# Summed weights made by VectorE instead of an adding DMA, the pre-norm weights loaded with x's first piece, and the products with v half a step later

## The chip, the cores and the metric

The kernel runs on one NeuronCore of a Trainium2 chip. The metric is the device time of one execution in microseconds (us). It was measured over several executions; one more was profiled, and its trace gives the rows below. Engines: TensorE (PE, its weight loads PEld), VectorE (DVE), ScalarE (ACT), GpSimd (POOL), and SyncE (SP), which here only issues DMAs.

## The reference

One encoder layer on 256 tokens of width 2048, all in float32. After a root-mean-square norm, one wide projection makes the inputs of a gated linear recurrence (branch A), of a windowed attention with 16 heads (branch B), of their gates and of two merge gates:

```python
xn = rms_norm(x, norm_pre_w[l])
z = xn @ w_in[l]
u_lru, g_lru, q, k, v, g_attn, m_lru, m_attn = jnp.split(z, split_at, axis=-1)
...
y_a = h.astype(x.dtype) * jax.nn.silu(g_lru)
...
y_b = windowed_gqa(q, k, v, attn_sink[l]) * jax.nn.silu(g_attn)
merged = (jax.nn.sigmoid(m_lru) * (y_a @ w_proj_a[l])
          + jax.nn.sigmoid(m_attn) * (y_b @ w_proj_b[l]))
x = x + rms_norm(merged @ w_out[l], norm_post_w[l])
```

`rms_norm` divides by the root of the mean square of a row and multiplies by a weight for each column.

## The kernel before

**Arithmetic.** A float32 product is made of three products of a reduced type: an operand is split into a high part (a cast, by ScalarE, L219 for weights, L148 for other tiles) and a low part (value minus high part, by VectorE, L221 and L149), and TensorE sums high x high, high x low and low x high (L225 to L227 and their relatives). So each weight passes DMA, ScalarE and VectorE before TensorE reads it.

**The order of the work** is written out by hand. `START`, `MERGE` and `OUT` are lists of steps, one per 128x2048 block of weights (1 MB). A name is a group letter, a part and an index: `p` and `b` are the products with `w_proj_a` and `w_proj_b`, `o` those with `w_out`, `u` and `v` parts of the first projection. A step has two halves of 128x1024. In the steps named by a small letter a half is a tick of the schedule; in the steps L, M, N, A and O both halves make one. The loop at L1136 goes through the halves; at half number hs it issues the work due at its tick, then the cast of half hs + 4, the subtraction of half hs + 3, then the matmuls of half hs. Each engine works through its own queue in that order. Weights land in three 1 MB buffers (`raw`), loaded three steps ahead by SP's queue.

**Seven products instead of eight.** Groups L, M, N, A and O (class `Seven`) compute two by two blocks of an output from seven block products. Some multiply a single block of the activations, some a sum of blocks, and the weights of some are sums too:

```python
    "m5": ("s1", "x", (0, 1)),
    "m3": ("s4", "y", (1, 1)),
    "m6": ("s2", "x", (1, 1)),
    "m7": ("s3", "y", (0, 1)),
    "m4": ("a22", "x", (1, 0)),
```

The second entry names a cell (two 128x1024 tiles a and b, for each half q of the contraction). A cell starts as one block of weights and other blocks are added one after the other: x is the block of m1, then that of m5, m6 and m4 are added; y is the block of m3, then m7's is added. So m6 adds to x the block (1, 1), which is also what y holds when m3 is split. In the kernel before, each addition is a DMA issued on POOL's queue that adds what it reads from DRAM to the tile (`load(..., add=True)`, L192), asked for five steps ahead (`lead == 5`, L374), after the previous value of the tile has been split. The tiles are named after group, cell and half: `Ax0a` is group A, cell x, q = 0, half a.

Groups A and O stand in these lists:

```python
    b0.0 Am5.1 b0.1 Am3.0 b0.2 b0.3 Am3.1 b1.0 Am6.0 b1.1 b1.2 Am6.1 b1.3 Am7.0 b2.0 b2.1 Am7.1 b2.2 Am4.0 b2.3 b3.0
OUT = """o2.0 o2.1 Om1.1 o2.2 Om5.1 Om2.0 o2.3 Om3.0 Om6.0 Om3.1 o3.0 Om6.1 Om2.1 o3.1 Om7.0 Om7.1 Om4.0 Om4.1
    o3.2 o3.3""".split()
```

**Behind a product pb** (steps b, `add_pb`), VectorE multiplies each token half of its sums by a gate and adds the other branch (L970 and L971, tile `sm`); one tick later TensorE transposes the result (`turn`, L982, tile `mt`), 128x128 at a time, which ScalarE and VectorE split for the last product. o2's sums are evacuated by ScalarE (L1080) and VectorE (L1085).

**Attention heads** (`head`) run beside the steps. Two heads share a transposition through DRAM: `send`, `fetch` (DMAs), `p_parts` (split into `ph` and `pl`), `values` (the six products with v, PSUM bank `o`), `gate_out` (VectorE, `sga`, L927); `yb_parts` splits the gated result for the pb products. Their ticks are offsets from the head's first tick: `p_parts` at 11, `values` at 13, `gate_out` at 14.

**Shared space.** SBUF tiles of 4 KB a partition come from a pool of 45 units; PSUM has four banks of one kind and two double banks of another.

**The start.** TensorE first spins on ones (`SPIN` matmuls, L449). ScalarE's queue issues the DMA of x's first 128 columns (transposed), then the first 16 columns of `pvec`, the pre-norm weights, then the second piece of x; SP's queue issues the other pieces of x and the first weights in small parts. `scale_x` (L479, L481) multiplies a piece of x by the norm's weights and splits it. The norm's division by the row's root comes later (`row_scale`, at tick 10), from the squares of the four tiles of x (`square`, L499); its result is kept in `rbc`.

Of the kernel before, what the change touches and what calls it, by code (L numbers as in the profile page):

```python
# [28 lines left out]
EPS = 1e-6  # L29
UNITS = 45  # L30
DECAY = 12
SPIN = 11
HEAD0 = -16
HEADS_AT = (0, 3, 5, 8, 11)
FIRST = 8
# [34 lines left out]
LRU = (-4, 0, 2, 2, 2, 2, 2, 4)  # L70
QUADS = {"u": ("w_in", U0), "v": ("w_in", V0), "p": ("w_proj_a", 0),
         "b": ("w_proj_b", 0), "o": ("w_out", 0)}
PAIRS = {"g": GL0, "h": GA0, "w": U0, "k": K0, "q": Q0}
SEVENS = {"L": ("w_in", ML0 + 1024), "M": ("w_in", ML0), "N": ("w_in", MA0), "A": ("w_in", MA0 + 1536), "O": ("w_out", 0)}


PV_NORM = 0
PV_CW = 16
PV_CB = PV_CW + 64
PV_BR = PV_CB + 16  # L80
PV_BI = PV_BR + 32
# [2 lines left out]
PV_N = PV_SINK + 16  # L84
# [28 lines left out]
    return {k: n for n, k in enumerate(dict.fromkeys(content(p) for p in load_plan()))}  # L113


def body(ctx, tc, x, xT, wall, wlru, pvec, npost, ident_d, mask_d, rope_d, out):
    nc = tc.nc
    const = ctx.enter_context(tc.tile_pool(name="const", bufs=1))
    units = ctx.enter_context(tc.tile_pool(name="units", bufs=UNITS))
# [35 lines left out]
    plan = load_plan()  # L155
# [6 lines left out]
    def at(hs, fn):  # L162
        assert hs >= now[0], (hs, now[0])
        due.setdefault(hs, []).append(fn)
# [15 lines left out]
    flat = lambda t: t.rearrange("p a b -> p (a b)") if len(t.shape) == 3 else t  # L180
# [15 lines left out]
    groups = {}  # L196
# [12 lines left out]
    def split(q, c=0, w=1024, cast=nc.scalar.copy, only=None):  # L209
        i, h = q // 2, q % 2  # L210
        if i >= len(plan):
            return
        if c == 0 and only != "l":
            parts[q] = [unit(f"w{s}{i}_{h}", F32R, (P, 1024)) for s in "hl"]
        wh, wl = parts[q]
        cell = groups[plan[i][1]].cell(*plan[i][2:]) if chained(i) else raws[i]
        hs, ls, raw = wh[:, c:c + w], wl[:, c:c + w], flat(cell[h])[:, c:c + w]
        if only != "l":
            cast(hs, raw)  # L219
        if only != "h":  # L220
            nc.vector.tensor_tensor(ls, raw, hs.bitcast(F32), ALU.subtract)  # L221

    def mm3(ps, wh, wl, xh, xl, start, stop, more=False):

# [118 lines left out]
    class Seven:  # L343
# [22 lines left out]
        def fetch(self, p, lead):  # L366
            m, q = p[2:]
            fresh = ("m1", "m3") if self.sums is None else ()
            if self.sums is None:
                if lead == 4 and m in fresh:  # L370
                    self.start(self.where(m), q)
                if lead == 4 and SEVEN[m][0][0] == "s":
                    self.kept[m, q] = x_sum(f"{self.name}{m}{q}", SEVEN[m][0], q)
            if lead == 5 and m in (("m5", "m6", "m7", "m4") if self.sums is None else ("m6", "m7", "m4")):  # L374
                load(self.cell(m, q), p, True)

        def start(self, where, q):
# [63 lines left out]
    pv = const.tile([P, PV_N], F32, name="pv")  # L441
# [5 lines left out]
    spin = bank("spin", (P, 512))  # L447
    for _ in range(SPIN):
        nc.tensor.matmul(spin[:, 0:P], ones, ones, start=True, stop=True)  # L449
    nc.gpsimd.memset(warm, 0.0)  # L450
    nc.gpsimd.memset(eps, EPS)
    norm = lambda k: pv[:, PV_NORM + k:PV_NORM + k + 1]
    ident = const.tile([P, P], F32, name="ident")
    rbc = const.tile([P, S], F32, name="rbc")

    xt = [unit(f"xT{i}") for i in range(4)]
    xs = []
    raw_tile(0)
    for j in range(4):
        (nc.scalar if j < 2 else nc.sync).dma_start(xt[0][:, j], xT[0, :, j])  # L460
        if j == 0:
            nc.scalar.dma_start(pv[:, 0:PV_CW], pvec[:, 0:PV_CW])
        nc.sync.dma_start(raws[0][j // 2][:, j % 2 * 512:(j % 2 + 1) * 512], wall[0, :, j * 512:(j + 1) * 512])
    for i in (1, 2):
        for j in (0, 2):
# [3 lines left out]
            for c in ((0, 512), (512, 1024)) if i == 1 else ((0, 1024),):  # L469
                nc.sync.dma_start(raws[i][j // 2][:, slice(*c)], wall[i, :, j * 512 + c[0]:j * 512 + c[1]])  # L470
    nc.sync.dma_start(xt[3], xT[3])
    nc.sync.dma_start(pv[:, PV_CW:PV_N], pvec[:, PV_CW:PV_N])
    nc.scalar.activation(warm, warm, AF.Sigmoid)

    def scale_x(i, j, between=lambda: None):
        if j % 2 == 0:
            xs.append(pair_unit(f"xs{2 * i + j // 2}"))
        h, l = xs[-1][:, j % 2, 0], xs[-1][:, j % 2, 1]
        nc.scalar.activation(h, xt[i][:, j], AF.Copy, scale=norm(4 * i + j))  # L479
        between()  # L480
        nc.vector.scalar_tensor_tensor(l, xt[i][:, j], norm(4 * i + j), h.bitcast(F32), ALU.mult, ALU.subtract)  # L481

    for j in range(4):
        if j == 0:
# [375 lines left out]
    def head(hd, qh, ql, b, both, end):  # L860

        g, j = hd // 4, hd % 4
        sk = pv[:, PV_SINK + hd:PV_SINK + hd + 1]
        ts = [slice(t * P, (t + 1) * P) for t in range(2)]
        v = {}

        def scores():
            v["sc"] = bank(f"sc{hd}")
            for t in range(2):
                mm3(v["sc"][:, t], qh[:, j, ts[t]], ql[:, j, ts[t]], kv["kh"][:, g], kv["kl"][:, g], True, True)  # L870

        def expo():
            p = v["p"] = half_unit(f"p{hd}", ("p", "uu")[hd % 2])
            sc = v.pop("sc")
            m, nm, es = tiny(f"m{hd}"), tiny(f"nm{hd}"), tiny(f"es{hd}")
            dn = v["dn"] = tiny(f"dn{hd}")
            for t in range(2):
                nc.vector.tensor_tensor_reduce(p[:, t], sc[:, t], table["mask"][:, t], rtok_sc[:, t:t + 1], sk, ALU.add, ALU.max, m[:, t:t + 1])
            nc.vector.tensor_scalar(nm, m, -1.0, None, ALU.mult)
            soon(lambda: exps(p, nm, es, dn))  # L880

        def exps(p, nm, es, dn):
            for t in range(2):
                nc.scalar.activation(p[:, t], p[:, t], AF.Exp, bias=nm[:, t:t + 1], accum_out=dn[:, t:t + 1])
            nc.scalar.activation(es, nm, AF.Exp, bias=sk)
            v["es"] = es

        def normalise():
            dn, rd = v["dn"], tiny(f"rd{hd}")
            nc.vector.tensor_tensor(dn, dn, v["es"], ALU.add)  # L890
            nc.vector.reciprocal(rd, dn)
            soon(lambda: [nc.scalar.activation(v["p"][:, t], v["p"][:, t], AF.Copy, scale=rd[:, t:t + 1]) for t in range(2)])

        def flip():

# [13 lines left out]

        def fetch():  # L910
            u = both["l"] = unit(f"pl{hd}", F32R, (P, 1024))
            nc.sync.dma_start(u.bitcast(F32), both.pop("d").rearrange("c i t a x -> (c i) (t a x)"))

        def p_parts():
            both["h"] = unit(f"ph{hd}", F32R, (P, 1024))
            parts_of(both["h"], both["l"], both["l"].bitcast(F32))

        def values():
            both["o"] = bank(f"o{hd}")
            ks = slice(g * P, (g + 1) * P)  # L920
            turned = [both[i].rearrange("p (a h k x) -> p h k a x", a=8, h=2, k=2) for i in "hl"]
            for kt in range(2):
                mm3(both["o"], kv["vh"][:, kt, ks], kv["vl"][:, kt, ks], *(t[:, :, kt] for t in turned), kt == 0, kt == 1)

        def gate_out():
            y = sga[g][:, j - 1:j + 1]
            nc.vector.tensor_tensor(y, both["o"], y, ALU.mult)  # L927
            both.clear()
            if j == 3 and g < 2:
                soon(lambda: park("yb", sga, g), 4)  # L930

        for d, fn in ((0, scores), (1, expo), (3, normalise), (5, flip)):
            at(b + d, fn)
        if j % 2 == 1:
            for d, fn in enumerate((send, None, fetch, None, None, p_parts, None, values, gate_out), 6):
                if fn:
                    at(b + d, fn)
            if g > 1:
                at(max(b + 15, end + hd // 2 - 4), lambda: yb_parts(hd // 2))

    def yb_parts(q):
        yb[q] = pair_unit(f"yb{q}")
        n = q % 2 * 2
        parts_of(yb[q][:, :, 0], yb[q][:, :, 1], sga[q // 2][:, n:n + 2])
# [125 lines left out]
    b, n = ticks(), ticks(len(plan))  # L1070
# [159 lines left out]
```

## Time and profile before

| | |
|---|---|
| runs before | 880.4 us median of 3 (878.27 to 880.61) |
| profiled execution | 880.26 us, span 878.5 us |
| mean granted TensorE clock | 0.995 |
| DMA moved | 252.12 MB, mean 287 GB/s |
| HBM read, written | 232.43 MB, 18.87 MB |

The span goes from the first to the last instruction of the kernel. Busy shares are averages over the whole span. In a row of a timeline stand the start (us from the span's start), the time, the engine, the line, the operation, the tiles as out<-in, the shape, the count, and in brackets the engine's idle time before it with what ended it. In a row of the waits stand engine, line and what was waited for, then the total in us, the count and the longest. A matmul's time in the trace overlaps the next one's. The times of DMAs are told as us from issue to landing.

### The profile page before, as it was taken

The page shows a single profiled execution, that of the slowest core. Times are in us where ns is not written, and L with a number is a line of the kernel's source. Part 1 is how long each engine was busy: PE and PEld are TensorE (multiplying, and loading weights), DVE is VectorE, ACT ScalarE, POOL GpSimd, SP SyncE. Part 2 cuts the span into 40 slices and gives each one's busy share as a digit, 9 for nine tenths or more (in the row PEclk, how much of TensorE's full clock was granted, in tenths as well). Part 3 has the DMA queues.
Part 4 walks back from the last instruction along what each step waited for, and adds up shares of the span by engine and source line. Part 5 has one row for each costly group of instructions (what it writes and reads, how often), then busy time and mean ns, then how long its engine had stood idle before and what let it go on. Part 6 is the DMA issues. An engine that isn't in the chain of part 4 may idle for free.

```text
span 878.5 us, 12340 instructions
## 1 busy us (share of the span) xinstructions
PE 867.7 (99%) x4480; PEld 744.2 (85%) x4480; DVE 720.4 (82%) x967; ACT 643.2 (73%) x929; POOL 72.7 (8%) x104
## 2 busy tenths in 40 slices
PE   9999999999999999999999999999999999999996
PEld 9888888888888888888888888788888788888885
DVE  6899999898897988889777788987688578777776
ACT  7689687977788796886877699976566456555654
POOL 0000000012000011100001100000001001000200
PEclk9999999999999999999999999999999999999998
DMA  8757699999959999986999987899989998999962
GB/s 333 273 192 248 197 370 236 369 323 290 332 180 307 317 283 316 303 323 210 269 361 304 309 269 259 313 333 292 324 324 324 345 300 246 304 288 391 247 177 96
DMA packets 64685, 252.12 MB, mean 287 GB/s; under 512 B 6512, under 2 KB 19568, under 8 KB 49136
## 3 DMA queue, kind: packets, MB, share of 16 engines
q1 hardware_dynamic: 52384, 208.59, 64.1%
q0 software_dynamic: 11520, 41.95, 24.4%
q10 hardware_dynamic: 720, 0.79, 0.3%
q8 instruction: 35, 0.57, 0.3%
q14 instruction: 26, 0.21, 0.1%
HBM read 232.43 MB, written 18.87 MB: 286 GB/s over the span
## 4 chain that ended last, share of the span: by engine, by line
PE 84%; ACT 5%; DMA 5%; issue 4%; DVE 2%; POOLq 0%; POOL 0%; ACTq 0%; DVEq 0%
PE ga L252 7%; PE gl L252 7%; PE u L252 5%; DMA raw<-wall_dram 5%; PE Mm L407 4%; PE Lm L407 4%; PE gl L250 3%; PE ga L250 3%; PE Am L407 3%; PE Om L407 3%; PE q L252 3%; PE pb__6875 L272 3%; PE u L250 3%; PE u_ps L550 3%; PE pa__6035 L272 2%
## 5 line engine op out<-in xcount | busy, mean ns | idle before, releaser
L221 DVE TENSOR_TENSOR wl<-raw,wh 128x1024 fp32r<-128x1024 f32 (+1 forms) x252 | 299.1, 1202 | 71.2 <-ACT wh L219 55.5
L219 ACT CAST wh<-raw 128x1024 fp32r<-128x1024 f32 (+1 forms) x251 | 253.7, 1036 | 77.1 <-DMA raw<-wall_dram 51.9
L252 PE MATMUL ga<-xs,wh 128*128 128x512 f32 x256 | 63.5, 391 | 0.0
L252 PE MATMUL gl<-xs,wh 128*128 128x512 f32 x256 | 63.4, 391 | 0.0
L252 PE MATMUL q<-xs,wh 128*128 128x512 f32 x256 | 63.2, 391 | 0.0
L252 PEld LDWEIGHTS gl<-xs,wh 128*128 128x128 f32 x256 | 47.0, 188 | 9.1
L252 PEld LDWEIGHTS q<-xs,wh 128*128 128x128 f32 x256 | 47.0, 188 | 9.0
L252 PEld LDWEIGHTS ga<-xs,wh 128*128 128x128 f32 x256 | 46.7, 188 | 8.8
L252 PE MATMUL u<-xs,wh 128*128 128x512 f32 x192 | 47.5, 391 | 0.0
L252 PEld LDWEIGHTS u<-xs,wh 128*128 128x128 f32 x192 | 35.2, 188 | 6.7
L250 PEld LDWEIGHTS q<-xs,wl 128*128 128x128 f32 x256 | 33.2, 191 | 1.2
L250 PE MATMUL q<-xs,wl 128*128 128x256 f32 x256 | 34.0, 283 | 0.0
L250 PEld LDWEIGHTS ga<-xs,wl 128*128 128x128 f32 x256 | 33.0, 191 | 1.2
L250 PEld LDWEIGHTS gl<-xs,wl 128*128 128x128 f32 x256 | 32.8, 191 | 1.2
L250 PE MATMUL ga<-xs,wl 128*128 128x256 f32 x256 | 33.5, 283 | 0.0
L250 PE MATMUL gl<-xs,wl 128*128 128x256 f32 x256 | 33.2, 283 | 0.0
L250 PEld LDWEIGHTS u<-xs,wl 128*128 128x128 f32 x192 | 24.6, 191 | 0.9
L250 PE MATMUL u<-xs,wl 128*128 128x256 f32 x192 | 24.9, 283 | 0.0
L655 DVE SCALAR_TENSOR_TENSOR uu<-upad,pv,uu 128x256 f32<-128x256 f32 x48 | 23.2, 483 | 1.7
L739 ACT ACTIVATE sig<-sg 128x512 f32<-128x512 f32 x16 | 10.2, 636 | 14.2 <-DVE sg L582 14.2
L272 PE MATMUL pb__6875<-wh,yb 128*128 128x512 f32 x64 | 18.4, 413 | 0.0
L227 PE MATMUL gate<-ul,lwl 128*128 128x256 f32 x64 | 18.1, 283 | 0.0
(502 smaller groups left out, 2085.5 us busy)
## 6 DMA issues: line engine op xcount, KB each, us to landing
raw<-wall_dram SPq DMA_DIRECT2D x121, 1024.0 KB, 7.9
lraw<-wlru_dram SPq DMA_DIRECT2D x8, 512.0 KB, 6.3
away<-xx SPq DMA_DIRECT2D x8, 512.0 KB, 8.3
Lm<-away SPq DMA_DIRECT2D x8, 512.0 KB, 12.3
Mm<-away SPq DMA_DIRECT2D x8, 512.0 KB, 13.6
Nm<-away SPq DMA_DIRECT2D x8, 512.0 KB, 14.5
turn<-pt SPq DMA_DIRECT2D x32, 128.0 KB, 4.6
pl<-turn SPq DMA_DIRECT2D x8, 512.0 KB, 7.8
```

Source lines behind the costliest of these rows:

```text
L219: cast(hs, raw)
L221: nc.vector.tensor_tensor(ls, raw, hs.bitcast(F32), ALU.subtract)
L227: nc.tensor.matmul(ps, wl, xh, start=False, stop=stop, skip_group_check=more)
L250: nc.tensor.matmul(ps[:, 1], wl[:, sl], a[:, 0], start=False, stop=False)
L252: nc.tensor.matmul(ps, wh[:, sl], a, start=k == 0, stop=k == KT - 1)
L272: nc.tensor.matmul(got[t], a[:, i], (wl if low else wh)[:, sl], start=k + low + i == 0, stop=low == 1 and k == KT - 1)
L407: nc.tensor.matmul(self.ps[b], a[i], (wl if low else wh)[:, sl], start=fresh and j + low + i == 0, stop=last and j + low == 2, skip_group_ ...
L550: nc.tensor.matmul(ups[b // 2][:, b % 2, m], w[:, sl], a[:, n], start=k == 0 and w is wh and m == 0, stop=stop)
L655: nc.vector.scalar_tensor_tensor(u, up[:, j, tap:tap + S], cw[:, tap:tap + 1], u, ALU.mult, ALU.add)
L739: nc.scalar.activation(sg, dst, AF.Sigmoid)
```

## The change

1. For groups A and O, m6's block is no longer added by DMA. When the half of m3 is split, VectorE also adds this half (the tile of cell y) to the tile of cell x, right behind the subtraction. Eight adding DMAs of 128x1024 fall away (A and O, q = 0 and 1, halves a and b) and eight VectorE additions of 128x1024 come in. Groups L, M and N stay as they are.
2. The 16 columns of pre-norm weights move from `pvec` into a new array `x0`, behind x's first 128 columns (transposed), so that one DMA of 272 columns brings both into a tile `piece`. Its first 256 columns are `rbc`, written only later by the norm. `scale_x` reads x's first piece there; GpSimd copies it into its place in `xT` for the squares. ScalarE's queue issues one DMA less. `pvec` is loaded whole, by the DMA that loaded its rest.
3. `SPIN` goes from 11 to 8.
4. `values` and `gate_out` move from 13 and 14 to 14 and 15 ticks behind the head's first, and the earliest tick of `yb_parts` from 15 to 16.

```diff
-SPIN = 11
+SPIN = 8
...
+ADDED = {'A': {'m3': 'm6'}, 'O': {'m3': 'm6'}}
...
-PV_NORM = 0
-PV_CW = 16
+PV_CW = 0
...
         if only != "h":
             nc.vector.tensor_tensor(ls, raw, hs.bitcast(F32), ALU.subtract)
+            if plan[i][0] == "part" and plan[i][2] in ADDED.get(plan[i][1], ()):
+                x = flat(groups[plan[i][1]].cells["x", plan[i][3]][h])
+                nc.vector.tensor_tensor(x, x, raw, ALU.add)
...
-            if lead == 5 and m in (("m5", "m6", "m7", "m4") if self.sums is None else ("m6", "m7", "m4")):
+            if lead == 5 and m in ("m5", "m6", "m7", "m4")[self.sums is not None:] and m not in ADDED.get(self.name, {}).values():
                 load(self.cell(m, q), p, True)
...
-    norm = lambda k: pv[:, PV_NORM + k:PV_NORM + k + 1]
-    rbc = const.tile([P, S], F32, name="rbc")
+    piece = const.tile([P, S + KT], F32, name="rbc")
+    rbc = piece[:, 0:S]
+    norm = lambda k: piece[:, S + k:S + k + 1]
...
     for j in range(4):
-        (nc.scalar if j < 2 else nc.sync).dma_start(xt[0][:, j], xT[0, :, j])
         if j == 0:
-            nc.scalar.dma_start(pv[:, 0:PV_CW], pvec[:, 0:PV_CW])
+            nc.scalar.dma_start(piece, x0)
+        else:
+            (nc.scalar if j == 1 else nc.sync).dma_start(xt[0][:, j], xT[0, :, j])
         nc.sync.dma_start(raws[0][j // 2][:, j % 2 * 512:(j % 2 + 1) * 512], wall[0, :, j * 512:(j + 1) * 512])
...
-    nc.sync.dma_start(pv[:, PV_CW:PV_N], pvec[:, PV_CW:PV_N])
+    nc.sync.dma_start(pv, pvec)
+    nc.gpsimd.tensor_copy(xt[0][:, 0], rbc)
...
-        nc.scalar.activation(h, xt[i][:, j], AF.Copy, scale=norm(4 * i + j))
+        src = xt[i][:, j] if i + j else rbc
+        nc.scalar.activation(h, src, AF.Copy, scale=norm(4 * i + j))
         between()
-        nc.vector.scalar_tensor_tensor(l, xt[i][:, j], norm(4 * i + j), h.bitcast(F32), ALU.mult, ALU.subtract)
+        nc.vector.scalar_tensor_tensor(l, src, norm(4 * i + j), h.bitcast(F32), ALU.mult, ALU.subtract)
...
-            for d, fn in enumerate((send, None, fetch, None, None, p_parts, None, values, gate_out), 6):
+            for d, fn in enumerate((send, None, fetch, None, None, p_parts, None, None, values, gate_out), 6):
                 if fn:
                     at(b + d, fn)
             if g > 1:
-                at(max(b + 15, end + hd // 2 - 4), lambda: yb_parts(hd // 2))
+                at(max(b + 16, end + hd // 2 - 4), lambda: yb_parts(hd // 2))
```

More of the change, by code (lines that the diff above doesn't have):

```diff
@@ L113, in wall_rows, with body @@
     return {k: n for n, k in enumerate(dict.fromkeys(content(p) for p in load_plan()))}
-def body(ctx, tc, x, xT, wall, wlru, pvec, npost, ident_d, mask_d, rope_d, out):
+def body(ctx, tc, x, x0, xT, wall, wlru, pvec, npost, ident_d, mask_d, rope_d, out):
     nc = tc.nc
@@ L1199 @@
     pvec = np.concatenate([
-        cols(v["norm_pre_w"][0], 16),
         v["conv_w"][0].reshape(4, 16, P).transpose(2, 1, 0).reshape(P, 64),
@@ L1211 @@
         "x": x,
+        "x0": np.concatenate([x.T[:P], cols(v["norm_pre_w"][0], 16)], axis=1),
         "xT": x.T.reshape(4, 4, P, S).transpose(0, 2, 1, 3),
```

## The prediction

> **What bounds the kernel now.** I read the page first, then the waits of TensorE, then the two places where it stood still. On the page TensorE is busy for 99% of the span, so the other engines matter only where they make it wait.
>
> ```profile
> PE 867.7 (99%) x4480; PEld 744.2 (85%) x4480; DVE 720.4 (82%) x967; ACT 643.2 (73%) x929; POOL 72.7 (8%) x104
> q1 hardware_dynamic: 52384, 208.59, 64.1%
> q0 software_dynamic: 11520, 41.95, 24.4%
> PE mt L982 <- DVE sm L971: 1.8, 2, 0.9
> PE o L226 <- DVE pl L149: 0.6, 1, 0.6
> ```
>
> The last two lines are all that TensorE waits for between its first spin and its last product: 1.8 us before transposes of the merged rows, 0.6 us before a product of the softmax weights with v. So what the change can gain is these waits, what follows from them, and the start.
>
> The first wait, in the timeline of TensorE:
>
> ```profile
> 696.97 1.07 PE L407 MATMUL Am<-wh,Am 128*128 128x512 f32 x4
> 700.76 0.44 PE L982 MATMUL mt<-ident,sm 128*128 128x128 f32 x2 [0.91 <-DVE sm L971]
> 702.09 0.44 PE L982 MATMUL mt<-ident,sm 128*128 128x128 f32 x2 [0.89 <-DVE sm L971]
> 702.28 1.62 PE L272 MATMUL pb__6875<-wh,yb 128*128 128x512 f32 x4
> ```
>
> Two waits of 0.91 and 0.89 us, and then four products that take 1.62 us. Views of stretches (columns: length, busy time and count of each engine, granted clock, DMA share, GB/s) say why, and what the DMA did before:
>
> ```profile
> 652.00:676.00 24.00, 24.00 (x107) 19.75 (x106) 19.82 (x23) 18.69 (x23) 3.49 (x4) 1.00 1.04 342
> 676.00:700.00 24.00, 23.85 (x106) 19.42 (x104) 13.33 (x13) 10.25 (x12) 3.49 (x4) 1.00 1.04 348
> 700.00:704.00 4.00, 2.35 (x9) 1.82 (x10) 3.96 (x5) 2.39 (x5) 0.00 (x0) 0.85 1.04 305
> 704.00:708.00 4.00, 4.00 (x14) 3.16 (x14) 3.93 (x7) 1.20 (x2) 1.76 (x2) 0.72 1.03 291
> ```
>
> The granted clock falls to 0.85 and 0.72 in two stretches of 4 us: 4 x 0.15 + 4 x 0.28 = 1.72 us of matmul time lost, as much as the waits themselves. Together the place costs 1.80 + 1.72 = 3.52 us. And all DMA engines are full (1.04) for the 48 us before it. The chain of waits and VectorE's timeline lead from the transposes back to a load:
>
> ```profile
> 668.49 2.72 PE pb__6627 L272 x12
> 676.88 20.11 DMA raw<-wall_dram
> 697.06 1.06 ACT wh L219
> 699.29 0.69 DVE sm L970
> ```
> ```profile
> 693.16 1.23 DVE L221 TENSOR_TENSOR wl<-Ay1a,wh 128x1024 fp32r<-128x1024 f32 x1 [1.52 <-ACT wh L219]
> 698.15 1.23 DVE L221 TENSOR_TENSOR wl<-raw,wh 128x1024 fp32r<-128x1024 f32 x1 [2.49 <-ACT wh L219]
> ```
>
> The weights of step b1.0 were asked for at 676.88 and landed 20.11 us later, at 697.0. ScalarE's cast and VectorE's subtraction (698.15) had to wait for them, and the multiplication that feeds the transposes stands behind this subtraction in VectorE's order: it could have begun when TensorE ended the product pb0 and went on to a step of Am (696.97, so about 697.1), and began at 699.29, 2.2 us late. So the stall is a late DMA, in a stretch where the DMA is full.
>
> **The change, part by part.**
>
> *Sums for m6 by VectorE, group A.* The four halves of m6 of group A are no longer loaded and added by DMA. They are issued on POOL's queue here, first and last of the four:
>
> ```profile
> 655.02 0.89 POOL L192 DMA_DIRECT2D Ax0a<-wall_dram  x1 [33.44 <-DVE wl L221]
> 673.19 0.86 POOL L192 DMA_DIRECT2D Ax1b<-wall_dram  x1 [4.62 <-DVE wl L221]
> ```
>
> All four stand ahead of or beside the load of 676.88. Their price: queue q0 took 24.4% of 878.5 us = 214.4 us of all 16 engines for 41.95 MB, that is 80 halves of 0.524 MB, 2.68 us each; q1 took 563.1 us for 208.59 MB, 1.42 us for as much. An added half costs nearly twice a plain one. Four of them: 10.7 us of full DMA time gone before 697. Since the DMA is full throughout, loads behind them can land up to 10.7 us sooner. What is needed is only the 2.2 us by which the multiplication was late: a fifth of the relief is enough. Bounds: 0 (the load lands no earlier) and 3.52 us. I take 3.4: next in line are the second token half's sums. VectorE does four operations of 0.69 us from 697.1 on and ends about 699.9, just when TensorE has done the twelve products of Am (2.72 us from 696.97) and comes to the transposes; I leave 0.1 us for that.
>
> *What VectorE does instead*: eight additions of 128x1024, four for A, four for O. The same operation on the same engine has these rows:
>
> ```profile
> 811.30 3.50 DVE L221 TENSOR_TENSOR wl<-raw,wh 128x1024 fp32r<-128x1024 f32 x3
> L221 DVE TENSOR_TENSOR wl<-raw,wh x61: 1180/1219/1227, 639.4 to 839.9; 128x1024 fp32r<-128x1024 f32 x61
> 825.58 0.69 DVE L1085 TENSOR_TENSOR yw<-o__7602,np 128x512 f32<-128x512 f32 x1 [1.55 <-ACT junk L1080]
> 828.45 0.68 DVE L1085 TENSOR_TENSOR yw<-o__7602,np 128x512 f32<-128x512 f32 x1
> 834.18 1.07 PE L272 MATMUL o<-wh,ms 128*128 128x512 f32 x4
> ```
>
> Three in a row take 3.50 us and one 1.22, so one more costs (3.50 - 1.22) / 2 = 1.14 us; eight: 9.1 us, VectorE from 720 to 730 us. On the path they cost nothing if these covers hold. In A the two additions of q = 1 stand behind the subtraction of 693.16 and its like for half b: 2.3 us, in front of VectorE's idle 2.49 us before 698.15, so they fit even if no load came sooner. In O they stand behind the four Oy subtractions. Queued behind them are the evacuations of o2, at 825.58 and 828.45; for it waits the second PSUM tile of o3, whose first product is at 834.18. Margin 834.18 - 829.13 = 5.05 us; four additions are 4.6 us at most. The casts of Ox now wait for VectorE, not for a DMA. The four O loads give back another 10.7 us of DMA time, but TensorE waits for none there: gain 0, with the cover that it makes up for the earlier pace. Without it the lateness would be that of a half, 2.68 us at most, before the loads behind it. POOL's next additions (m7) wait 1.1 us more each for VectorE's reading of y, in front of a queue that is shorter by 10.7 us.
>
> *The products with v half a step later.*
>
> ```profile
> 565.67 0.40 PE L225 MATMUL o<-ph,vh 128*128 128x512 f32 x1
> 566.66 0.51 PE L226 MATMUL o<-pl,vh 128*128 128x512 f32 x1 [0.59 <-DVE pl L149]
> 565.38 1.23 DVE L149 TENSOR_TENSOR pl<-pl,ph 128x1024 fp32r<-128x1024 f32 x1
> L149 DVE TENSOR_TENSOR yb<-sga,yb x4: 679/684/684, 672.7 to 679.6; 128x512 fp32r<-128x512 f32 x4
> L272 PE MATMUL pb__6627<-wh,yb x64: 389/389/397, 668.3 to 696.3; 128*128 128x512 f32 x64
> ```
>
> TensorE came to the product at 565.67, its low part was ready at 566.6. Half a step (twelve products, 2.7 us) later TensorE comes at about 568.4, 1.8 us after it. The wait of 0.59 us goes; the clock did not fall after it, so that is all: bounds 0 and 0.59, I take 0.59. Moved with it, eight times: six products, one VectorE multiplication, a PSUM bank and two SBUF units held 2.7 us longer, and twice the store of yb on SP's queue. The last yb (started at 679.6) is ready some 2.7 us later, about 683, and its first use is the last half step of pb0, which begins 2.7 us before 696.97. Nothing of that is on the path; uncovered, a unit held longer takes at most half a step, 2.7 us, from a cast's lead.
>
> *The start.* The first weights of x no longer wait for a second small DMA.
>
> ```profile
> 0.75 0.41 ACTq L460 DMA_DIRECT2D xT<-xT_dram  x1
> xT<-xT_dram ACTq DMA_DIRECT2D x1, 128.0 KB, 3.5
> 1.19 0.45 ACTq L462 DMA_DIRECT2D pv<-pvec_dram  x1
> pv<-pvec_dram ACTq DMA_DIRECT2D x1, 8.0 KB, 4.0
> 1.00 5.06 PE L449 MATMUL spin<-ones 128*128 128x128 f32 x22 [1.00 <-POOL eps L451]
> 5.23 0.51 ACT L479 ACTIVATE xs<-xT,pv 128x256 fp32r<-128x256 f32 x1 [1.58 <-DMA pv<-pvec_dram]
> 21.61 1.05 ACT L219 CAST wh<-raw 128x1024 fp32r<-128x1024 f32 x1 [0.28 <-DMA raw<-wall_dram]
> 24.59 1.23 DVE L221 TENSOR_TENSOR wl<-raw,wh 128x1024 fp32r<-128x1024 f32 x1 [0.67 <-ACT wh L219]
> 24.92 2.17 PE L550 MATMUL u_ps<-xs,wl 128*128 128x256 f32 x16
> ```
>
> x's first piece was asked for at 0.75 and landed 3.5 us later, at 4.25; pv, asked for at 1.19, at 5.2. So the scaling can begin at about 4.3, 0.9 us sooner, and eight spins end at 1.00 + 8 x 0.46 = 4.7, just before the first product (4.85). But the gain doesn't last: in the group of 24.92 the second eight products use the low weights that VectorE finishes at 24.59 + 1.23 = 25.82, while TensorE reaches them at 25.87. That subtraction goes back through ScalarE's order (cast, square, cast, each 1.05) to a landing at 21.6, before which ScalarE idled 0.28 us. An earlier start turns into waits there unless the landing comes sooner, and the DMA loses only 8 KB of work. Bounds 0 and 0.9; I take 0.1. POOL's new copy of x's first piece is used by the first square, after 15 us.
>
> By the Trainium skill (TensorE: Matmul & The Clock Gate, Part 1) the clock is released only by a free-running window of about 3.4 us of sustained activity. Eight spins are 3.7 us, so by that rule the release could slip by a window; that is the third rival below.
>
> **Sum.** 3.4 + 0.59 + 0.1 = 4.1 us. The profiled execution took 880.26 us, 0.1 below the median of the runs (880.4): 880.26 - 4.1 = 876.2 us.
>
> **Rivals.**
> 1. *The relief does not reach the load* (or reaches it by less than 2.2 us): the queue refills with loads that are asked for sooner. For it: the DMA stays at 1.04 after 700, too. Against: the removed halves are a fifth of the 48 us ahead. Then 880.26 - 0.7 = 879.6, or 877.9 if only the clock's fall is spared.
> 2. *The start passes through*: the landing at 21.6 moves with everything else. For it: ScalarE idles 0.28 us before it. Against: the DMA, full by then, sets it. 876.2 - 0.8 = 875.4.
> 3. *The clock is released late at the start*: a stretch as after 702, 1.72 us lost, of which 0.9 is covered by the earlier start: 876.2 + 0.8 = 877.0. Against: products follow the spins within 0.2 us.
> 4. *Slower: VectorE falls behind in O.* Place: the second half of o3.0 at 834.18. If an addition costs far more than 1.14 us, because POOL issues four loads in this very stretch, the evacuation of o2 comes after its margin of 5.05 us plus VectorE's idle 1.5. It decides from 1.65 us per addition. At twice 1.2 us: 9.7 - 6.6 = 3.1 us of wait and, after a wait of that size, 1.7 us of clock: 876.2 + 4.8 = 881.0. Against: 61 operations of this shape, beside POOL's issues or not, all took 1.18 to 1.23 us.
>
> **How the numbers follow.** Forecast 0.64, rival 1 0.15, rivals 2 and 3 0.06 each, rival 4 0.09. The likeliest case has 875.3 (the start gives all, no remainder) to 877.1 (one wait of 0.9 left). The three runs before lie 2.3 us apart, and the range reaches half way into rival 1: 874.8 to 878.8. A measurement of this kernel tells 0.3%, 2.6 us, from no change. Faster: 0.64 + 0.12 = 0.76; within: 0.15; slower: 0.09.
>
> **What would show it.** Right: no wait of mt on sm near 697, clock 1.00 in that stretch, the raw load of b1.0 landing before 694; no wait of o on pl; the first product at about 4.9, and new waits of TensorE before 26 us that eat 0.8 of it; q0 with 72 halves, 37.7 MB. Wrong: TensorE waiting for wl or for PSUM after 818, VectorE's additions over 1.3 us, or the clock below 1 after 10 us.

## The result and the profile after

The kernel after takes 876.76 us (median of ten, 876.38 to 877.71); the kernel before, on the same chip in turn with it, 879.22 us (median of ten, 878.03 to 883.28). The ratio is 0.9970, with a 95% interval of 0.9957 to 0.9983: 2.5 us less. The profiled execution took 876.50 us (span 874.7 us, mean clock 0.998) where that of before took 880.26 us: 3.76 us less. The page of the kernel after and all that TensorE waits for (engine, line, what for; total, count, longest):

```profile
PE 864.9 (99%) x4474; PEld 741.7 (85%) x4474; DVE 728.6 (83%) x975; ACT 643.1 (74%) x929; POOL 66.1 (8%) x97
q1 hardware_dynamic: 52384, 208.59, 64.6%
q0 software_dynamic: 10368, 37.75, 22.2%
PE spin L452 <- POOL eps L454: 1.0, 1, 1.0
PE u_ps L557 <- ACT xs L486: 0.5, 1, 0.5
PE u_ps L557 <- ACT wh L219: 0.3, 1, 0.3
```

The waits of `mt` and of `o` are gone; two new ones, 0.46 and 0.26 us, stand in the first eight microseconds. Queue q0 carries 72 halves. The place of the stall, in the timelines of TensorE, VectorE and ScalarE of the kernel after:

```profile
698.59 0.62 PE L410 MATMUL Am<-wl,Am 128*128 128x512 f32 x2
699.04 0.71 PE L989 MATMUL mt<-ident,sm 128*128 128x128 f32 x4
699.51 1.17 PE L275 MATMUL pb__6872<-wh,yb 128*128 128x512 f32 x4
687.52 1.22 DVE L224 TENSOR_TENSOR Ax1a<-Ax1a,Ay1a 128x1024 f32<-128x1024 f32 x1
689.79 1.22 DVE L224 TENSOR_TENSOR Ax1b<-Ax1b,Ay1b 128x1024 f32<-128x1024 f32 x1
690.93 1.22 DVE L221 TENSOR_TENSOR wl<-raw,wh 128x1024 fp32r<-128x1024 f32 x1
696.52 0.69 DVE L977 TENSOR_TENSOR sm<-pb__6624,sm 128x512 f32<-128x512 f32 x1 [4.37 <-PE pb__6624 L275]
687.87 2.00 ACT L219 CAST wh<-raw 128x1024 fp32r<-128x1024 f32 x2 [1.18 <-DMA raw<-wall_dram]
```

The weights of b1.0 are cast at 687.87, on landing; in the kernel before this cast began at 697.06. So of the 10.7 us that the load could gain, it gained 9.2. Its subtraction (690.93) no longer stands in front of the gate's multiplication: VectorE waits 4.37 us for TensorE there, where it came 2.2 us late before, and the four transposes follow the products without a gap. The same stretches as before (length, busy time and count of PE, PEld, DVE, ACT, POOL; clock, DMA share, GB/s):

```profile
652.00:676.00 24.00, 24.00 (x107) 19.75 (x106) 20.46 (x23) 18.76 (x23) 0.00 (x0) 1.00 0.96 369
676.00:700.00 24.00, 24.00 (x109) 19.80 (x108) 19.56 (x21) 11.45 (x13) 3.48 (x4) 1.00 1.01 301
700.00:704.00 4.00, 4.00 (x19) 3.27 (x19) 3.93 (x7) 2.45 (x4) 1.76 (x2) 1.00 1.04 407
704.00:708.00 4.00, 4.00 (x21) 3.32 (x20) 2.61 (x4) 2.29 (x5) 0.00 (x0) 1.00 0.99 232
```

The clock stays at 1.00. The DMA is hardly less full (0.96 and 1.01 against 1.04): the freed time went into loads that come sooner, and the share doesn't show it. The start, in the timelines of the kernel after, and the first and last of the products of v0 to v3 in the groups of both kernels (ns least, median, most; start of the first and of the last), after first:

```profile
1.00 3.55 PE L452 MATMUL spin<-ones 128*128 128x128 f32 x16 [1.00 <-POOL eps L454]
5.01 1.26 PE L557 MATMUL u_ps<-xs,wh 128*128 128x256 f32 x8 [0.46 <-ACT xs L486]
21.98 1.05 ACT L219 CAST wh<-raw 128x1024 fp32r<-128x1024 f32 x1 [0.66 <-DMA raw<-wall_dram]
L275 PE MATMUL v_ps<-wh,xs x64: 387/389/586, 29.1 to 50.7; 128*128 128x512 f32 x64
```
```profile
L272 PE MATMUL v_ps<-wh,xs x64: 389/389/577, 28.8 to 50.3; 128*128 128x512 f32 x64
```

The first product stands at 5.01 us; in the trace of before it stands at 5.79, behind the longer spins. Yet the first product with v0's weights stands at 29.14, 0.38 us later than before (28.76): the load of the fourth block landed at 21.96, not 21.59, and ScalarE idled 0.66 us for it. With this the difference between these two profiled executions closes: 1.80 + 1.72 + 0.59 - 0.38 = 3.73 of the 3.76 us. The 0.38 belongs to this pair of executions, though. In the seven profiles with the old start (before and six of the runs below) v0's first product stands at 28.8 to 30.8 us, and that of before is the earliest; in the four with the new start as changed here it stands at 29.1 to 29.5. So the profiles don't show that the new start comes out later.

### The profile page after: what moved, and what is told of

Same layout as the page of the kernel before. It is cut to its first block, busy times and chain, and to the rows that moved or that the text cites. A ratio compares the mean times of both kernels' runs of the same rounds, so it can differ in the third digit from the quotient of the medians.

```text
span 874.7 us, 12312 instructions
## 1 busy us (share of the span) xinstructions
PE 864.9 (99%) x4474; PEld 741.7 (85%) x4474; DVE 728.6 (83%) x975; ACT 643.1 (74%) x929; POOL 66.1 (8%) x97
## 4 chain that ended last, share of the span: by engine, by line
PE 94%; issue 3%; DMA 2%; ACT 0%; POOLq 0%; DVE 0%; SPq 0%; ACTq 0%
PE ga L255 7%; PE q L255 7%; PE gl L255 7%; PE u L255 5%; PE Am L410 4%; PE Mm L410 4%; PE Lm L410 4%; PE Nm L410 4%; PE ga L253 3%; PE q L253 3%; PE gl L253 3%; PE Om L410 3%; PE u L253 3%; PE pa__6025 L275 2%; PE pa__5514 L275 2%
## 5 line engine op out<-in xcount | busy, mean ns | idle before, releaser
L148 ACT CAST ms<-mt 128x512 fp32r<-128x512 f32 x8 | 4.7, 588 | 20.0 <-PE mt L989 20.0
```

What stands on the lines that cost most here:

```text
L148: nc.scalar.copy(h, src)
```

## The experiments

Each was run in turn with the kernel before, 5 to 12 times; the ratio is to that.

| run | what | median us | before | ratio (95%) |
|---|---|---|---|---|
| a_only | VectorE's sums in A alone | 877.32 | 879.32 | 0.9967 (0.9955 to 0.9979) |
| v_only | products with v later, alone | 879.92 | 879.32 | 1.0002 (0.9989 to 1.0015) |
| head_only | the new start alone | 879.73 | 879.32 | 0.9998 (0.9987 to 1.0010) |
| no_head | all but the new start | 876.62 | 879.32 | 0.9959 (0.9945 to 0.9972) |
| a_and_v | sums in A, v later | 876.36 | 879.23 | 0.9970 (0.9958 to 0.9982) |
| half_dose | sums in A for q = 0 alone, v later | 876.52 | 879.23 | 0.9971 (0.9961 to 0.9982) |
| plain | A's adding DMAs made plain writes, v later | 876.20 | 879.23 | 0.9966 (0.9954 to 0.9979) |
| no_adds | after, VectorE's eight additions left out | 877.06 | 879.23 | 0.9972 (0.9964 to 0.9981) |
| start2 | after, with an altered start | 875.90 | 880.54 | 0.9949 (0.9937 to 0.9962) |
| start2_a | the same, sums in A alone | 875.45 | 880.54 | 0.9943 (0.9930 to 0.9957) |
| after_again | after | 877.25 | 880.54 | 0.9964 (0.9951 to 0.9977) |
| start2_an | altered start, sums in A and N | 875.38 | 881.12 | 0.9942 (0.9928 to 0.9956) |

### The parts alone

Theory: the stall in A is worth 1.8 us and more, and the DMA relief of A's four halves removes it. Rivals: the start, or the later products with v, brought the gain.

**The sums in A alone**, in the kernel before:

```diff
+ADDED = {'A': {'m3': 'm6'}}
```

> Before with group A's four adding halves made by VectorE, nothing else changed. Theory (A's relief of the DMA is what removes the stall at the transposes): no wait of mt on sm, clock 1.00 in that stretch, the load of b1.0 lands before 694 us; the wait of o on pl (0.6 us) stays; about 2.2 us below the kernel before. Rival (it takes all eight halves, or the products with v as well): the wait of mt stays at over 1 us and the time is within 0.7 us of before.

All that TensorE waits for in this run, and ScalarE's cast of the fourth block's first half:

```profile
PE u_ps L554 <- ACT wh L220: 1.0, 1, 1.0
PE spin L453 <- POOL eps L455: 1.0, 1, 1.0
PE o L230 <- DVE pl L150: 0.6, 1, 0.6
23.66 1.04 ACT L220 CAST wh<-raw 128x1024 fp32r<-128x1024 f32 x1 [1.04 <-DMA raw<-wall_dram]
```

By the medians 2.0 us of the 2.5 come from this part: no wait of `mt`, while the wait of `o` is where it was. The profiled execution is the slowest of the ten (879.05 us): the fourth block is cast 2.05 us later than in the profile of before (23.66 and 21.61), and v0's first product stands at 30.8 us, 2.1 later. The start alone thus differs by that much between executions.

**The products with v alone:**

```diff
-                at(max(b + 15, end + hd // 2 - 4), lambda: yb_parts(hd // 2))
+                at(max(b + 16, end + hd // 2 - 4), lambda: yb_parts(hd // 2))
```
(and one more `None` ahead of `values` in the list of the head's steps)

> Before with the products with v half a step later, nothing else. Theory (the stall behind is set by a DMA that does not come sooner): the wait of o on pl (0.6 us) goes, and TensorE waits 0.6 us longer at the transposes instead (1.8 to 2.4 us in all): 0.0 us. Rival (the two waits add up as in the prediction's sum): mt's waits stay at 1.8 us and the time falls by 0.6 us.

TensorE's waits in this run:

```profile
PE mt L982 <- DVE sm L971: 1.7, 2, 0.9
PE sc L227 <- DVE ql L149: 1.4, 1, 1.4
PE spin L449 <- POOL eps L451: 1.0, 1, 1.0
```

The wait of `o` went, the stall in A stayed at 1.7 us (the theory had 1.8 to 2.4), and the time is that of before. But the profile also has a wait that the profile of before doesn't have: 1.4 us at 503 us, before the first products of the heads, where nothing is moved yet. There a load of weights in group N's stretch is cast on landing at 494.61; in the profile of before, at 491.49 (ScalarE, first this run, then before):

```profile
494.61 1.05 ACT L219 CAST wh<-raw 128x1024 fp32r<-128x1024 f32 x1 [7.29 <-DMA raw<-wall_dram]
```
```profile
491.49 1.05 ACT L219 CAST wh<-raw 128x1024 fp32r<-128x1024 f32 x1 [4.92 <-DMA raw<-wall_dram]
```

The same late load shows in one other profile below (half_dose, 1.0 us of wait), and 0.59 us is within the interval. So the run doesn't tell whether the stall in A takes the 0.59 us back. It tells that the part alone brings nothing that can be measured.

**The new start alone:**

```diff
-SPIN = 11
+SPIN = 8
...
+            nc.scalar.dma_start(piece, x0)
```

> Before with the new start (one DMA for x's first piece and the weights, 8 spins), nothing else. Theory (DMA sets the pace of the start): the first product at about 5.0 us, 0.8 sooner, but the last group of the first four steps (u0.3, second half) at 25.8 to 26.3 us as before: 0.0 to 0.4 us slower at that place, and the total within 0.5 us of before. Rival (the later landing of the fourth weights in the profile of the changed kernel was chance): that group at 25.8 us, total 0.1 us below before.

Nothing that can be told: 0.9998. Its profile has the first product at 4.93 us, the fourth block landing at 22.04, the low weights of u0.3's second half reached at 26.32 (with a wait of 0.30 us for VectorE's subtraction) and v0's first product at 29.2. That is the theory's place, to within 0.02 us. But the old start's own landings lie between 21.6 and 23.6 us, so whether the landing moved by the new start isn't decided.

**All but the new start** (the kernel after with `SPIN` at 11, `x0` and `piece` taken back):

> The changed kernel with the old start and 11 spins. Theory (the new start costs what its profile shows at the last group of the first four steps, 26.24 against 25.87 us): 0.4 us below the changed kernel, 2.8 us below before. Rival (the start is worth nothing either way): as the changed kernel, 2.5 us below before. In both no wait of mt on sm.

876.62 us beside 877.32 of the sums in A alone: the two other parts (v later, and O) bring 0.7 us on top of A's, close to the 0.59 us of the wait of `o`; the two intervals overlap, so this is no proof. The run is 2.7 us below before, between the theory's 2.8 and the rival's 2.5, and doesn't decide between them.

### How much relief it takes, and of what kind

**A and v, without O:**

```diff
-ADDED = {'A': {'m3': 'm6'}, 'O': {'m3': 'm6'}}
+ADDED = {'A': {'m3': 'm6'}}
```
(and the old start)

> Before with group A's halves by VectorE and the products with v half a step later; group O and the start as before. Theory (O's four halves are worth nothing, since TensorE never waits there): as the version that has O as well (876.6 us), 2.7 us below before, no wait of mt or o. Rival (O's relief is needed once TensorE comes sooner): a wait of TensorE after 780 us and at least 0.5 us more.

The ratio, 0.9970, is that of the kernel after, and TensorE waits for nothing behind the spins. Within the interval O's four neither help nor harm.

**Half of A's additions**, those of q = 0:

```diff
-            if plan[i][0] == "part" and plan[i][2] in ADDED.get(plan[i][1], ()):
+            if plan[i][0] == "part" and plan[i][2] in ADDED.get(plan[i][1], ()) and plan[i][3] == 0:
```

> As the version with A and the later products with v, but only q = 0 of m6 by VectorE; q = 1 stays two adding DMAs. That is 5.4 us of DMA time less in place of 10.7. Theory (2.2 us are needed): still no wait of mt on sm, b1.0's load lands before 694 us, the same time (876.6 us). Rival (the whole relief is needed): waits of mt of 0.5 us or more, 1 us slower.

ScalarE's cast of b1.0's weights and TensorE at the transposes, with two adding DMAs fewer instead of four:

```profile
694.31 2.00 ACT L220 CAST wh<-raw 128x1024 fp32r<-128x1024 f32 x2 [5.80 <-DMA raw<-wall_dram]
700.40 0.62 PE L411 MATMUL Am<-wl,Am 128*128 128x512 f32 x2
700.86 0.71 PE L986 MATMUL mt<-ident,sm 128*128 128x128 f32 x4
```

No wait. b1.0's load landed at 694.2, 2.8 us sooner than in the profile of before; 5.4 us were the most that it could gain, and the 2.2 that were missing are enough. The forecast of a landing before 694 is missed by 0.2 us. In this profile TensorE also comes about 1.4 us later to this place (v0's first product is 1.0 us later and it waits 1.0 us at 503, while the 0.59 of `o` is gone), which widens the margin; the median of the runs, 876.52, shows no loss either.

**The same transfers, but as plain writes.** The four halves of m6 of A stay on POOL's queue, with their bytes, and overwrite the tile instead of adding to it; VectorE adds nothing.

```diff
-                load(self.cell(m, q), p, True)
+                load(self.cell(m, q), p, (self.name, m) != ("A", "m6"))
...
-                nc.sync.dma_start(flat(cell[h]), w[:, h * 1024:(h + 1) * 1024])
+                (nc.sync if add is None else nc.gpsimd).dma_start(flat(cell[h]), w[:, h * 1024:(h + 1) * 1024])
```

> Before with the later products with v, and group A's four halves of m6 loaded by the same queue at the same place, but written over the tile and not added to it: as many bytes, and m6 of group A takes the block (1,1) alone in place of the sum. Theory (an adding half takes 2.68 us of all engines, a plain one 1.42, so 5.0 us are relieved, and that is enough): no wait of mt on sm, 876.6 us. Rival (what counts is the bytes, or POOL's issue): the waits of mt stay at 1.5 us or more, 879.3 us.

Queue q0, the stretches, ScalarE's cast of b1.0's weights and the transposes:

```profile
q0 software_dynamic: 11520, 41.95, 23.9%
652.00:676.00 24.00, 24.00 (x107) 19.75 (x106) 21.00 (x23) 18.66 (x23) 2.15 (x4) 1.00 1.03 408
676.00:700.00 24.00, 24.00 (x109) 19.81 (x108) 14.72 (x17) 11.01 (x12) 3.50 (x4) 1.00 1.04 336
691.39 2.00 ACT L219 CAST wh<-raw 128x1024 fp32r<-128x1024 f32 x2 [4.48 <-DMA raw<-wall_dram]
699.26 0.72 PE L982 MATMUL mt<-ident,sm 128*128 128x128 f32 x4
```

The DMA is as full as before (1.03 and 1.04), but it moves 408 GB/s in the first stretch where it moved 342 (336 and 348 in the second), and the stall is gone: b1.0's weights are cast at 691.39. So what was in the way is the price of adding, not the bytes: 4 x (2.68 - 1.42) = 5.0 us by the shares of the queues. Queue q0, with the same bytes, took 23.9% of 874.4 = 209.0 us here and 214.4 before: 5.4 us less. The load came 5.7 us sooner.

**VectorE's eight additions left out** of the kernel after:

```diff
-                nc.vector.tensor_tensor(x, x, raw, ALU.add)
+                pass
```

> The changed kernel without VectorE's eight additions: m6 of groups A and O takes the sum without its last block. Theory (VectorE's 9.1 us are hidden): as the changed kernel, 2.5 us below before, within 0.3 us of it. Rival (they hold something up): faster than the changed kernel by 0.5 us or more.

The two stretches ahead of the transposes without the additions (VectorE is the figure after PEld's):

```profile
652.00:676.00 24.00, 24.00 (x107) 19.75 (x106) 20.27 (x23) 19.05 (x23) 0.00 (x0) 1.00 0.95 371
676.00:700.00 24.00, 24.00 (x110) 19.76 (x109) 15.21 (x17) 11.25 (x12) 3.48 (x4) 1.00 1.00 297
```

35.5 us against 40.0 of the kernel after, and no gain in time (877.06 us, 2.2 below before): VectorE's 9.8 us (8 x 1.22) are hidden.

### The start, and a faster version

In the kernel after ScalarE waits for the fourth block of weights. The next two runs change what stands before it:

```diff
+            if i == 3:
+                for h in range(2):
+                    nc.sync.dma_start(t[:, h], w[:, h * 1024:(h + 1) * 1024])
...
-    nc.sync.dma_start(pv, pvec)
+    at(1, lambda: nc.sync.dma_start(pv, pvec))
...
-        at(i, lambda i=i: square(i))
+        at(2 + i, lambda i=i: square(i))
```

> The kernel after, with three edits at the start: the fourth block of weights is loaded as two DMAs of 512 KB instead of one of 1 MB, the DMA of pvec is issued at the second tick instead of before the first blocks, and each of the squares (ScalarE) comes two ticks later, so that none stands between the two casts of that block. Theory (the landing of the fourth block, and ScalarE's order behind it, eat what the earlier first product gives): its first half lands at 19 to 20 us instead of 21.96, the second half step of the fourth step (26.24 us after, counted to its products with the low weights) is reached at 25.0 to 25.6 us, and the kernel takes 0.6 to 1.2 us less than the kernel after: about 875.7 where that one takes 876.7. Rival (the start is bound by something later, the square roots or the steps behind, and a gain there is lost before 60 us): the same time as the kernel after, within 0.3 us. A new wait would show where the row scale is wanted, at tick 10, if the squares come too late for it.

> The same start as in the run before, and VectorE's additions in group A alone: m6 of group O is added by DMA as in the kernel before. Theory (the four additions of O are worth nothing either way): the same time as with them, within 0.4 us, about 875.7. Rival (the relief of O counts for something once the rest is out of the way): 0.5 us or more slower than the run with both groups.

> The kernel after, unchanged, on the same chip as the two runs with the altered start. Theory: 876.4 to 877.0 us, mean granted clock 0.998 in every run, no wait of TensorE at the transposes of the merged rows. The kernel before shows a mean clock of 0.995 in about a fifth of its runs, and these take some 1.7 us more than its others; if a run of the kernel after showed 0.995 too, the fall would not hang on that stall.

The fourth block in the first of them, ScalarE and TensorE:

```profile
21.24 1.05 ACT L224 CAST wh<-raw 128x1024 fp32r<-128x1024 f32 x1 [0.84 <-DMA raw<-wall_dram]
22.19 1.06 ACT L511 ACTIVATE sq<-xT 128x1024 f32<-128x1024 f32 x1
23.16 1.03 ACT L224 CAST wh<-raw 128x1024 fp32r<-128x1024 f32 x1
L280 PE MATMUL v_ps<-wh,xs x64: 387/389/586, 28.4 to 50.0; 128*128 128x512 f32 x64
```

By the medians the altered start is 1.35 us faster than the kernel after in the same series (875.90 beside 877.25), and with sums in A alone 1.8 us; the fastest runs lie closer (875.69 and 875.24 beside 876.21). Without O's additions the time is 0.45 us lower, a little more than the 0.4 of the theory and not the way of the rival. The kernel after itself spread further in this series than expected, up to 878.55, at a clock of 0.997 and 0.998 throughout. The mechanism is only half right: the first half landed at 21.2, not 19 to 20, and a square still stands between the two casts, since the shift by two ticks put an earlier square there. v0's first product came 0.7 us sooner than in the kernel after, yet the profiled execution is only 0.27 us shorter (876.23 and 876.50). In the profile of the second, TensorE waits 0.7 us for a scaled piece of x at the very start, then runs its first products at about half pace (the rows stand in the last section), v0's first product stands at 29.8, and the execution takes 876.6, the slowest of its five. So the profiles explain a part of the gain; which of the three edits makes it was not tried one by one.

**Group N as well.** The late load of the v run lies in N's stretch, so the same remedy was put there:

```diff
-ADDED = {'A': {'m3': 'm6'}}
+ADDED = {'A': {'m3': 'm6'}, 'N': {'m3': 'm6'}}
```

> The altered start with VectorE's additions in groups A and N (N in place of O: the block of m6 of N is added by VectorE too, four adding DMAs between 490 and 520 us fall away and four additions of 1.22 us come in). In the profiles of the run with v moved alone and of the run with half of A's additions TensorE waited 1.4 and 1.0 us at 503 us for the low part of q, behind a weight load of group N that landed near 494.6 us; in the profiles of before and after the same load lands at 491.5 and nothing waits. Theory (a removed adding DMA is worth something only where TensorE waits for what it delays): without a steady wait in N the median stays that of the same kernel without N's additions, 875.5 us within 0.5, and the spread shrinks if that late load is what spreads the runs. Rival 1: the late load of N costs something in most runs, then about 0.5 to 1 us less, 874.5 to 875.0. Rival 2: VectorE, busy with the heads there, falls behind by the four additions (4.6 us) and TensorE waits for low parts near 500 us: 0.5 us or more above 875.5.

875.38 us (875.17 to 876.05) beside 875.45 in the other series: nothing that can be told, as the theory has it. The relief did reach its place: the cast that waits 4.78 us for this load in the profile of start2_a and begins at 492.40 begins at 487.21 here, without a wait for the load. Nothing on TensorE's path needed it. The medians of this run and of start2_a are the lowest of all.

### The fall of the clock

Stretches of about 3.41 us, the first of each pair over the stall, in the profiles of before, of the new start alone and of v alone, and v alone's transposes. In the third pair no fall marks the place; it is reckoned back from the clock's fall at the kernel's end (873.72 us) in 50 and 51 steps of 3.413 us, as it comes out for before (873.46 - 50 x 3.413 = 702.8):

```profile
699.37:702.79 3.42, 1.62 (x9) 0.92 (x8) 3.35 (x6) 1.81 (x3) 0.00 (x0) 1.00 1.04 308
702.79:706.20 3.41, 3.41 (x9) 2.63 (x8) 3.41 (x5) 2.41 (x4) 1.24 (x2) 0.50 1.03 281
```
```profile
699.35:702.76 3.41, 1.55 (x9) 0.85 (x8) 3.34 (x6) 2.01 (x3) 0.00 (x0) 1.00 1.03 306
702.76:706.18 3.42, 3.42 (x11) 2.65 (x10) 3.42 (x4) 2.64 (x4) 0.88 (x1) 0.50 1.04 289
```
```profile
699.64:703.05 3.41, 2.01 (x9) 1.16 (x8) 3.34 (x5) 2.55 (x3) 0.00 (x0) 1.00 1.04 320
703.05:706.46 3.41, 3.15 (x15) 2.63 (x16) 3.41 (x4) 2.65 (x4) 0.53 (x1) 1.00 1.03 287
```
```profile
701.99 0.44 PE L982 MATMUL mt<-ident,sm 128*128 128x128 f32 x2 [0.77 <-DVE sm L971]
703.31 0.44 PE L982 MATMUL mt<-ident,sm 128*128 128x128 f32 x2 [0.89 <-DVE sm L971]
```

In the first two, TensorE is busy for 1.62 and 1.55 us of one window, and the next window of 3.41 us runs at half clock: 1.7 us lost. In the third the two waits are nearly as long (0.77 and 0.89 us), but the window ends before the second does and holds a longer run of products ahead of the first; it is busy for 2.01 us, and the clock stays. So by these three profiles the price of the same stall depends on where a window begins. The place of the third window is reckoned and not seen, and where between 1.62 and 2.01 us the border lies is open. How often it is paid is seen in the mean clock of the runs: 0.995 in 14 of 65 runs of before and in 4 of 24 of the two other kernels with the stall, and in none of 76 runs of the kernels without it. In three of the four series of before the runs at 0.995 took 1.8 to 1.9 us more than the others at the median; in the fourth, with two such runs, they did not.

## Why the prediction was right, and where its size was off

- **The sums in A.** Right in its mechanism, step by step: the adding DMAs cost 2.68 us each, the load of b1.0 came 9.2 us sooner, the waits of `mt` went, and no remainder of 0.1 was left. The quick proof is the plain writes: with the bytes left in place and only the adding taken away, the stall goes too.
- **The clock's fall, the term that was mis-sized.** The prediction counted 1.72 us whole, since the profiled execution had it. Of the 65 later runs of before, 14 have the mean clock that goes with it; at 0.22 x 1.7 it is worth 0.4 us on the average (an estimate) and next to nothing at the median. The profiled execution repaid it in full, hence 3.76 us there beside 2.5 between the medians.
- **The products with v.** The wait of 0.59 us is gone in every run with this part, and no_head beside a_only gives 0.7 us, with overlapping intervals. Alone it brought nothing that could be told. So the wait is shown to go, and what it is worth in time is argued from its size.
- **The start.** 0.1 us forecast; what it is worth can't be told from 0. The reason held: the landing that ScalarE waits for didn't come sooner (21.96 after, 21.59 before), and at 26.24 us TensorE's weight load waits 0.28 us for the low weights that the prediction named. But this place didn't eat the whole lead. The first product stands 0.78 us sooner than before, behind a wait of 0.46 us for the scaled x. A wait of 0.26 us at 7.14 is part of what follows; at 8.67 us (9.06 before) 0.39 of the lead is left, at 21.13 us (21.26 before) 0.13.
- **VectorE's additions and O.** 1.22 us each, where 1.14 was forecast; hidden, as no_adds shows. O's relief brings nothing that can be told, as a_and_v shows.
- **The sum.** 1.80 + 0.59 and 0.1 to 0.4 for the clock is 2.5 to 2.8 us, with a start that can't be told from 0; 2.5 were measured where 4.1 were forecast. The forecast of 876.2 us started from a profiled execution of 880.26, 1.0 above the median of 879.22 that the later series gave. A gain 1.6 us too large from a point 1.0 us too high ends 0.6 us from the measured 876.76: that the time came out so near is in part luck.
- **Rivals.** 1 (the relief doesn't reach the load) is refuted by the cast at 687.87; half of the relief would have done. 2 (the start passes through) is refuted by the landing, which didn't come sooner, and by v0's first product at 29.1 us here and 29.2 in head_only; the time of head_only, with an interval of 1.1 us below to 0.9 above before, couldn't refute it alone. 3 (the clock is released late at the start) is not refuted: in the profiled execution the pace behind the spins is nearly full, but in other executions it isn't (last section), and in after_again this cost nothing, as v0's first product stands at 29.14 there too. 4 (VectorE falls behind in O) is refuted: the additions in O took 1.22 us each, and TensorE's products wait for nothing after 8 us.
- **What would show it.** The signs named as right came: b1.0's landing before 694, clock 1.00 near 697, 72 halves on q0, the first product at 5.01 us for 4.9, new waits near the start, though not in the amounts forecast. None of the signs named as wrong came in the profile of the kernel after: its clock falls below 1 only behind the last product.

By the Trainium skill (TensorE: Matmul & The Clock Gate, Part 1) the window that decides the clock is 3413 ns long and free-running; the trace agrees, with half-clock stretches of 3.41 us and a fall that depends on the window's place. The same page of the Trainium skill (Why this matters for your kernels) asks for no idle gaps over about 3 us between bursts of products; here gaps of 0.91 and 0.89 us with two short transposes between were enough, and the measurement decides.

## What to carry to other kernels

Where the DMA is full, ask what a transfer costs in DMA time, not in bytes: an adding DMA took 2.68 us where a plain one took 1.42, and an addition of 1.22 us on VectorE, busy for 83% of the span, cost nothing here. Such relief was worth something only where TensorE waited for what was delayed: four halves in A gave 2 us, four in O and four in N nothing that could be told. And before a loss seen in one profile is put into a sum, look at how many runs have it: the mean clock of each run told that the half clock came in about a fifth of them.

## What was not expected of the hardware

**TensorE's pace at the start differs between executions, and the clock's column doesn't tell it.** The first eight products of 128x256 took 1.26 us in the profile of the kernel after (row of 5.01 us above). The same in after_again and in start2_a, two later groups of eight in start2_a, and the stretch of 5 to 10 us there (columns as above):

```profile
4.98 1.95 PE L557 MATMUL u_ps<-xs,wh 128*128 128x256 f32 x8 [0.20 <-ACT xs L486]
5.49 2.08 PE L562 MATMUL u_ps<-xs,wh 128*128 128x256 f32 x8 [0.70 <-ACT xs L491]
8.22 1.68 PE L562 MATMUL u_ps<-xs,wh 128*128 128x256 f32 x8
10.21 1.12 PE L562 MATMUL u_ps<-xs,wh 128*128 128x256 f32 x8
5.00:10.00 5.00, 4.51 (x23) 4.51 (x24) 4.32 (x9) 4.01 (x9) 0.55 (x5) 1.00 1.01 363
```

The first eight take 2.08 us in start2_a, nearly twice the 1.12 that such a group takes at 10.21; the group at 8.22 still takes 1.68. Yet the profile gives a granted clock of 1.00 for all of this time. So the mean clock of a run says nothing on the first microseconds. In after_again the slow group is made up for before v0's first product. In start2_a it isn't: v0's first product stands 1.4 us later than in start2, half of it from the first wait and half from the pace.

**The issue of a DMA at the start waits for the landing of an earlier one.** At the start of the kernel after, SP's queue issued its 15th to 19th DMA just as the one eight places earlier on the queue had landed (us, read from the trace), and the profile puts the wait of the last down to a landing (second block):

```
issued   8.82   9.48   10.15   10.81   12.49
landing of the eighth before
         8.80   9.47   10.13   10.78   12.41
```
```profile
SPq L207 <- DMA raw<-wall_dram: 1.0, 1, 1.0
```

The kernel before has the same pattern (its last: issued 12.47, landing 12.39). The last one is the load of the fourth block of weights: it was asked for at 12.5 in both kernels, although the first product had moved up by 0.8 us. But an earlier issue alone doesn't bring an earlier landing: in after_again this load was asked for at 11.93 and landed at 21.96 all the same, so the issue is not shown to be what stops the start's gain. The profile infers such waits from semaphores, which are the program's; that the chip's queue has a limit of eight is not shown.
